# RMS norms of a diffusion backbone: the root's transpose reads a token's value by a stride of zero, and for queries and keys ScalarE writes the wide tile

## The chip, the cores and the metric

The kernel runs on one core of one Trainium2 chip. The time is the device time of one execution in microseconds (us); of several runs the median is given. The engines of the core work side by side, each through its own queue in order: TensorE (PE in the profile, its weight loads PEld), VectorE (DVE), ScalarE (ACT), GpSimd (POOL) and SyncE (SP), which issues the DMA transfers.

## The reference

Two layers over 512 latent tokens and 256 context tokens of width 1024, all in float32. Layer 0 is grouped-query attention with 16 query heads and 4 key/value heads of 64, layer 1 a bidirectional Mamba-2 mixer; a gated convolution FFN follows each. Every sub-layer begins with an RMS norm over the 1024 features of a token, and queries and keys are normed once more, over the 64 features of each head:

```python
def rms_norm(x, g):
    xf = x.astype(jnp.float32)
    y = xf * lax.rsqrt(jnp.mean(xf * xf, axis=-1, keepdims=True) + EPS)
    return (y * g.astype(jnp.float32)).astype(x.dtype)

q_l = rms_norm(q_l.reshape(bsz, seq, N_HEADS, HEAD_DIM), q_norm)
k_l = rms_norm(k_l.reshape(bsz, seq, N_KV_HEADS, HEAD_DIM), k_norm)
...
h_l = modulate(rms_norm(x, norm_ffn_w[i]), mod_l[3], mod_l[4])
```

The change concerns only how the reciprocal root of the mean square is brought from one number per token to a row that can be multiplied with the features.

## The kernel before

Activations lie transposed: features on the 128 partitions, tokens along the free dimension. A product of full float32 precision is three fast products of split operands (`split`, `mm3`): a high part rounded by ScalarE (L85), the rest by VectorE or GpSimd (L87), and on TensorE high with high, high with low, low with high (L105, L106, L108). TensorE is fed in this way from the first to the last stage: projections of queries, keys and values, attention by pairs of heads, output projection, FFN of layer 0, the Mamba mixer, FFN of layer 1.

`rstd_rows` is the common helper of all the norms. It takes the squares `sq`, sums them over the partitions with TensorE (tile `ss…`: tokens now on the partitions, `c` columns per block of 128 tokens; `c` is 1 for the norms over 1024 and 2 for a pair of heads), and works out the root on tiny tiles of 128 x (blocks times `c`): VectorE makes the mean plus epsilon (`a`, called `rsa` in the profile, L239), ScalarE the power -1/2 by a logarithm and an exponential (`y`, `rsy`, L241), VectorE a Newton step (`u`, `rsu`, L243 and L244). The last operation of the Newton step (L247) is done on VectorE at full width: it reads `u` and `y` with a stride of zero and writes `rb…`, a tile in which every value is repeated 128/c times. TensorE transposes `rb` in blocks of 128 x 128 (L253, into `rsT…`); each block comes out with the tokens along the free dimension and the value repeated over the partitions, so that it can be multiplied with the features.

The helper runs 21 times: for the attention input (`rsTa`, latent and context), for 2 pairs of key heads and 8 pairs of query heads over all 768 tokens (`rsTq`; called from `normed`, L529 to L540), in three segments each for the FFN of layer 0 and the Mamba input (`rsTf`, `rsTs`), once behind the Mamba scan (`rsTy`) and in two segments for the FFN of layer 1 (`rsTf`).

The order on the engines comes from a scheduler that simulates the program with its own costs, except in the first 60 us, where it is written by hand. Each engine then takes its instructions strictly in that order. Generators put the work of queries ahead of the pair that needs it: `normed` squares the query on ScalarE (L529), scales it (L530), swaps halves for the rotation by four DMAs (L533), rotates on VectorE or GpSimd (L534 to L536), and multiplies by `rsTq` (L540); ScalarE then splits it into `qh` (L85). In a pair, TensorE makes scores `ps_s` (L674, L676), ScalarE their exponential `pr` (L677), TensorE the products with the values `ps_o` (L638); for the next pair TensorE makes raw scores `ps_m` (L602), whose row maxima VectorE takes (L604). `ps_s` and `ps_m` share two PSUM buffers, used in turn.

Of the kernel before, what the change touches and what calls it, by code (L numbers as in the profile page):

```python
# [7 lines left out]
P = 128  # L8
# [3 lines left out]
ALU = mybir.AluOpType  # L12
# [55 lines left out]
def t3(g, name, dt=F32, n=T):  # L68
    return g.t3p.tile([P, n], dt, tag="t3", bufs=g.n3, name=name)
# [145 lines left out]
def follow(g, bi):  # L215

    if g.last_act is not None:
        g.tc.add_manual_dep(bi.ins, g.last_act.ins.name, mybir.DependencyInfo(
            mybir.DependencyClass.NoSync, mybir.DependencyReason.DATA), reason="order of tables")
    g.last_act = bi  # L220
# [6 lines left out]
def rstd_rows(g, sq, n, cols, width, name, bank):  # L227

    nc = g.nc
    c = cols.shape[-1]
    nt = n // P
    ps = bank(f"ss{name}")
    for t in range(nt):
        nc.tensor.matmul(ps[:, t * c : (t + 1) * c], sq[:, t * P : (t + 1) * P], cols, start=True, stop=True)
    small = lambda nm: g.p.tile([P, nt * c], F32, tag="rst", bufs=8, name=nm)
    a, y, u = small("rsa"), small("rsy"), small("rsu")
    nc.vector.tensor_scalar(a, ps[:, : nt * c], 1.0 / width, EPS, ALU.mult, ALU.add)  # L239

    for f in ((lambda: nc.scalar.activation(y, a, AF.Ln)), (lambda: nc.scalar.activation(y, y, AF.Exp, scale=-0.5))):  # L241
        follow(g, f()) if g.tables else f()
    nc.vector.tensor_tensor(u, y, a, ALU.mult)  # L243
    nc.vector.scalar_tensor_tensor(u, y, -0.5, u, ALU.mult, ALU.mult)  # L244
    rb = t3(g, f"rb{name}", n=n)
    wide = lambda v: v.unsqueeze(2).broadcast_to([P, nt * c, P // c])
    nc.vector.scalar_tensor_tensor(rb.rearrange("p (a b) -> p a b", b=P // c), wide(u), 1.5, wide(y), ALU.add, ALU.mult)  # L247
    yield BREAK
    out = []
    for t0 in range(0, nt, 4):  # L250
        pt = bank(f"rsT{name}")
        for t in range(t0, min(nt, t0 + 4)):
            nc.tensor.transpose(pt[:, (t - t0) * P : (t - t0 + 1) * P], rb[:, t * P : (t + 1) * P], g.ident)  # L253
        yield (pt, t0 * P, min(n, (t0 + 4) * P))


# [53 lines left out]
class Norm:  # L310
# [23 lines left out]
    def gen(self, seg, x, lag=2):  # L334

        i, a, b = seg
        g, nc, n = self.g, self.g.nc, b - a
        for _ in range(lag):
            yield
        rows = rstd_rows(g, self.acc[seg, 6], n, g.ones[:, :1], D, self.name, lambda nm: Bank(g, nm))  # L340
        next(rows)
        for _ in range(lag):
            yield
        rs = t3(g, f"rs{self.name}", n=n)
        nc.scalar.copy(rs, next(rows)[0][:, :n])
        for m in range(KT):
            modulated(g, self.h[i][m], x[i], rs, a, b, *self.a, self.streams[i][1], m,
                      pool=m in ((1, 4) if a else (1, 3, 5, 7)))
            yield
# [30 lines left out]
def attention(g, fill, X, late):  # L380
# [57 lines left out]
    for m in range(KT):  # L438
        sq = t2("sql") if m else acc
        nc.scalar.activation(sq, xs[0][m], AF.Square)  # L440
        if m:
            nc.vector.tensor_tensor(acc, acc, sq, ALU.add)
    norm = rstd_rows(g, acc, L, g.ones[:, :1], D, "a", Bk)
    g.qn8 = g.const.tile([P, 1], F32, name="qn8")
    nc.vector.tensor_scalar(g.qn8, g.par[:, PC["qn"] : PC["qn"] + 1], HD ** -0.5, None, ALU.mult)
# [23 lines left out]
    for m in range(KT):  # L469
# [11 lines left out]
        if m == 3:  # L481
            norm = rstd_rows(g, sqc, C, g.ones[:, :1], D, "a", Bk)
            next(norm)
# [960 lines left out]
```

## Time and profile before

| | us |
|---|---|
| median of 3 runs | 1902.63 |
| lowest and highest of them | 1900.31, 1909.34 |
| the profiled execution | 1901.6 |
| its span, first to last instruction | 1899.8 |
| VectorE's wide writes at L247 for queries and keys: 10 of 128 x 768 | 10.7 in all |
| the other eleven writes at L247 | 6.1 in all |
| TensorE idle in the span | 35.7 |

In the profile's rows a time comes first, then a duration, the engine, the line, the operation, the output and inputs by the program's names, and the shape. Brackets at the end give how long the engine sat idle before the instruction and what ended that idle time. Lines of groups give the busy time in us, the mean duration of one in ns, and the idle time before them.

### The profile page before, as it was taken

Reading aid. Unit: us, or ns where it says so; the run is one execution under the profiler, and the core shown is the slowest. Engines: PE = TensorE matmul, PEld = TensorE weight load, DVE = VectorE, ACT = ScalarE, POOL = GpSimd, SP = SyncE. Lnnn points to the kernel's source line nnn. Section 1 sums busy time; section 2 is a strip of 40 time slices with the busy share of each in tenths; the row PEclk is TensorE's granted clock in tenths of the full one; section 3 lists DMA queues with packets and bytes.
Section 4 is the critical chain, followed back from the end, with each engine's and each line's share of the span. In section 5 each row is a group of like instructions: output and inputs, shape, how many; then the busy total and the mean of one; then the engine's idle time right before and its main releaser. Section 6 shows DMA issues by size and latency. Waiting matters only on the chain.

```text
span 1899.8 us, 28697 instructions
## 1 busy us (share of the span) xinstructions
PE 1864.1 (98%) x11426; PEld 1548.5 (82%) x11426; DVE 1313.6 (69%) x1949; ACT 820.2 (43%) x1420; POOL 308.8 (16%) x268
## 2 busy tenths in 40 slices
PE   9899999999999999999999999999999999999999
PEld 7775564688888888888888888888887878888887
DVE  6578778678777776444487877777788466565555
ACT  4635344254222222222266676776666352323331
POOL 2241111040000000000041334444333210000000
PEclk9999999999999999999999999999999999999999
DMA  9221341014433553122223334434453223323232
GB/s 340 84 84 45 115 142 67 34 50 176 153 123 120 190 188 135 67 67 67 67 86 115 118 89 122 123 113 132 122 153 107 85 78 97 98 83 111 89 100 89
DMA packets 73430, 210.10 MB, mean 111 GB/s; under 512 B 8912, under 2 KB 14416, under 8 KB 73168
## 3 DMA queue, kind: packets, MB, share of 16 engines
q1 hardware_dynamic: 73296, 208.26, 33.7%
q8 instruction: 90, 1.47, 0.3%
q14 instruction: 44, 0.36, 0.1%
HBM read 198.79 MB, written 6.82 MB: 108 GB/s over the span
## 4 chain that ended last, share of the span: by engine, by line
PE 79%; DVE 10%; issue 4%; ACT 2%; DMA 2%; POOL 1%; SPq 0%; POOLq 0%; DVEq 0%; ACTq 0%
PE ps_up L106 10%; PE ps_up L108 10%; PE ps_up L105 10%; PE ps_d L105 6%; PE ps_d L106 6%; PE ps_d L108 6%; PE ps_in L108 4%; PE ps_in L106 4%; PE ps_in L105 4%; PE ps_o L638 2%; PE ps_s L674 2%; PE ps_st L1034 2%; DVE ht L281 1%; PE ps_wo L108 1%; PE ps_wo L105 1%
## 5 line engine op out<-in xcount | busy, mean ns | idle before, releaser
L87 DVE TENSOR_TENSOR wl<-wst,wh 128x1024 fp32r<-128x1024 f32 x205 | 258.1, 1259 | 238.7 <-PE ps_up L106 128.2
L85 ACT CAST wh<-wst 128x1024 fp32r<-128x1024 f32 x211 | 221.2, 1049 | 407.3 <-DMA wst<-in_wup 330.3
L106 PE MATMUL ps_up<-hlf,wh 128*128 128x512 f32 (+1 forms) x1008 | 357.0, 354 | 0.0
L108 PE MATMUL ps_up<-hhf,wl 128*128 128x512 f32 (+1 forms) x1008 | 356.8, 354 | 0.0
L105 PE MATMUL ps_up<-hhf,wh 128*128 128x512 f32 x1008 | 356.8, 354 | 0.0
L106 PEld LDWEIGHTS ps_up<-hlf,wh 128*128 128x128 f32 x1008 | 190.6, 189 | 26.4
L105 PEld LDWEIGHTS ps_up<-hhf,wh 128*128 128x128 f32 x1008 | 190.5, 189 | 26.5
L108 PEld LDWEIGHTS ps_up<-hhf,wl 128*128 128x128 f32 x1008 | 190.5, 189 | 26.3
L105 PE MATMUL ps_in<-hhs,wh 128*128 128x512 f32 (+1 forms) x560 | 204.4, 365 | 1.2 <-ACT dt L919 1.2
L106 PE MATMUL ps_in<-hls,wh 128*128 128x512 f32 (+1 forms) x560 | 199.3, 356 | 0.0
L108 PE MATMUL ps_in<-hhs,wl 128*128 128x512 f32 (+1 forms) x560 | 198.7, 355 | 0.0
L105 PE MATMUL ps_d<-hdh,wh 128*128 128x512 f32 (+1 forms) x568 | 193.4, 342 | 0.2 <-ACT hdh L85 0.2
L108 PE MATMUL ps_d<-hdh,wl 128*128 128x512 f32 (+1 forms) x568 | 193.5, 341 | 0.0
L106 PE MATMUL ps_d<-hdl,wh 128*128 128x512 f32 (+1 forms) x568 | 192.9, 340 | 0.3 <-DVE hdl L87 0.3
L785 DVE SCALAR_TENSOR_TENSOR X<-ps_d,mod,X 128x512 f32<-128x512 f32 (+1 forms) x224 | 124.3, 583 | 35.0 <-PE ps_d L108 34.8
L105 PEld LDWEIGHTS ps_in<-hhs,wh 128*128 128x128 f32 x560 | 105.9, 189 | 16.4 <-ACT dt L919 1.4
L106 PEld LDWEIGHTS ps_d<-hdl,wh 128*128 128x128 f32 x568 | 106.7, 188 | 14.8 <-DVE hdl L87 0.7
L108 PEld LDWEIGHTS ps_in<-hhs,wl 128*128 128x128 f32 x560 | 105.8, 189 | 14.7
L108 PEld LDWEIGHTS ps_d<-hdh,wl 128*128 128x128 f32 x568 | 106.7, 188 | 13.1
L105 PEld LDWEIGHTS ps_d<-hdh,wh 128*128 128x128 f32 x568 | 106.3, 188 | 13.6 <-ACT hdh L85 0.7
L106 PEld LDWEIGHTS ps_in<-hls,wh 128*128 128x128 f32 x560 | 106.0, 189 | 13.2
L677 ACT ACTIVATE pr<-ps_s 128x1024 f32<-128x1024 f32 x56 | 57.2, 1022 | 107.1 <-PE ps_s L676 106.2
(338 smaller groups left out, 3536.8 us busy)
## 6 DMA issues: line engine op xcount, KB each, us to landing
wst<-in_wup SPq DMA_DIRECT2D x88, 512.0 KB, 3.3
wada<-in_adaT SPq DMA_DIRECT2D x56, 512.0 KB, 3.4
wst<-in_win SPq DMA_DIRECT2D x48, 512.0 KB, 3.5
wst<-in_wdown SPq DMA_DIRECT2D x44, 512.0 KB, 3.7
E<-ad SPq DMA_DIRECT2D x64, 256.0 KB, 6.5
wada<-in_adaB SPq DMA_DIRECT2D x24, 512.0 KB, 4.2
ec<-ead SPq DMA_DIRECT2D x64, 128.0 KB, 5.2
wst<-in_wout SPq DMA_DIRECT2D x16, 512.0 KB, 3.4
```

Of the source, the lines that this page charges most:

```text
L85: keep(nc.scalar.copy(hi, src))
L87: keep(eng.tensor_tensor(lo, src, _r(hi), ALU.subtract))
L105: mm(out, wh, ah, start=first, stop=False)
L106: mm(out, wh, al, start=False, stop=False)
L108: mm(out, wl, ah, start=False, stop=last)
L281: nc.vector.scalar_tensor_tensor(t[:, c0:c1], ap, g.moda[layer][ca][:, m, v : v + 1], rs[:, c0:c1], ALU.mult, ALU.mult)
L638: nc.tensor.matmul(po[S64[e], :n], v, pr[:, 512 * e + off : 512 * e + off + n], start=first, stop=last)
L674: nc.tensor.matmul(outs[e], a[S64[e], k], b[S64[e], q], start=i == 0, stop=False)
L677: nc.scalar.activation(pr, ps, AF.Exp)
L785: nc.vector.scalar_tensor_tensor(ap, o[:, c0:c1], gate[:, m, v : v + 1], ap, ALU.mult, ALU.add)
L1034: nc.tensor.matmul(ps[:, d * 256 : (d + 1) * 256], Bt[:, t * P : (t + 1) * P], xw[d][t], start=t == ts[0], stop=t == ts[-1])
```

## The change

The Newton step's last operation becomes as small as the others: it writes the result into `a`, 128 x (blocks times `c`). Where `c` is 1, the transpose reads the column of `a` for a block of 128 tokens with a stride of zero, 128 times the same value, so no wide tile is written or allocated. Where `c` is 2 (queries and keys), the wide tile `rb` stays, and ScalarE writes it by a copy that reads `a` with a stride of zero (L248 of the changed kernel).

```diff
     nc.vector.tensor_tensor(u, y, a, ALU.mult)
     nc.vector.scalar_tensor_tensor(u, y, -0.5, u, ALU.mult, ALU.mult)
-    rb = t3(g, f"rb{name}", n=n)
-    wide = lambda v: v.unsqueeze(2).broadcast_to([P, nt * c, P // c])
-    nc.vector.scalar_tensor_tensor(rb.rearrange("p (a b) -> p a b", b=P // c), wide(u), 1.5, wide(y), ALU.add, ALU.mult)
+    nc.vector.scalar_tensor_tensor(a, u, 1.5, y, ALU.add, ALU.mult)
+    if c > 1:
+        rb = t3(g, f"rb{name}", n=n)
+        nc.scalar.copy(rb.rearrange("p (a b) -> p a b", b=P // c), a.unsqueeze(2).broadcast_to([P, nt * c, P // c]))
     yield BREAK
-    out = []
     for t0 in range(0, nt, 4):
         pt = bank(f"rsT{name}")
         for t in range(t0, min(nt, t0 + 4)):
-            nc.tensor.transpose(pt[:, (t - t0) * P : (t - t0 + 1) * P], rb[:, t * P : (t + 1) * P], g.ident)
+            nc.tensor.transpose(pt[:, (t - t0) * P : (t - t0 + 1) * P],
+                                a[:, t : t + 1].broadcast_to([P, P]) if c == 1 else rb[:, t * P : (t + 1) * P], g.ident)
         yield (pt, t0 * P, min(n, (t0 + 4) * P))
```

Lines below the edit move down by one. The scheduler also moves other instructions. Three places follow; names ending in a number are buffers, whose numbers differ between the two programs.

ScalarE in the first pair of heads, from its first exponential `pr` on. Here the root of the query in `raw_902` (before) is worked out while the query in `raw_903` (before) is squared. Before:

```order
L677 ACTIVATE pr<-ps_s 128x1024
L85 CAST wh<-wst 128x1024
L241 ACTIVATE rsy<-rsa 128x12
L241 ACTIVATE rsy<-rsy 128x12
L529 ACTIVATE qsq<-raw_903 128x768
L677 ACTIVATE pr<-ps_s 128x1024
L530 ACTIVATE raw_903<-raw_903,qn_241 128x768
L241 ACTIVATE rsy<-rsa 128x12
```

The same place after the change:

```order
L678 ACTIVATE pr<-ps_s 128x1024
L85 CAST wh<-wst 128x1024
L241 ACTIVATE rsy<-rsa 128x12
L241 ACTIVATE rsy<-rsy 128x12
L248 COPY rbq<-rsa 128x768
L530 ACTIVATE qsq<-raw_901 128x768
L678 ACTIVATE pr<-ps_s 128x1024
L531 ACTIVATE raw_901<-raw_901,qn_241 128x768
L241 ACTIVATE rsy<-rsa 128x12
```

The new copy stands directly behind the root's exponential and ahead of the next query's square and of the second `pr`. GpSimd just before that place, before the change (rotation of a query, then two low parts of weights):

```order
L534 TENSOR_TENSOR raw_902<-raw_902,cs 128x512
L535 TENSOR_TENSOR qsw<-qsw,cs 128x512
L536 TENSOR_TENSOR raw_902<-raw_902,qsw 128x512
L87 TENSOR_TENSOR wl<-wst,wh 128x1024 x2
L534 TENSOR_TENSOR raw_903<-raw_903,cs 128x512
```

and after it:

```order
L535 TENSOR_TENSOR raw_900<-raw_900,cs 128x512
L536 TENSOR_TENSOR qsw<-qsw,cs 128x512
L87 TENSOR_TENSOR wl<-wst,wh 128x1024
L537 TENSOR_TENSOR raw_900<-raw_900,qsw 128x512
L87 TENSOR_TENSOR wl<-wst,wh 128x1024
L535 TENSOR_TENSOR raw_901<-raw_901,cs 128x512
```

The first of the two weight operations has moved ahead of the rotation's last step.

ScalarE where the third pair of heads ends and the fourth begins, before:

```order
L647 ACTIVATE y<-ps_sum 128x512
L241 ACTIVATE rsy<-rsa 128x12
L648 ACTIVATE y<-y 128x512
L241 ACTIVATE rsy<-rsy 128x12
L85 CAST qh<-qs 128x768
L677 ACTIVATE pr<-ps_s 128x1024
L647 ACTIVATE y<-ps_oc 128x256
```

and after:

```order
L648 ACTIVATE y<-ps_sum 128x512
L241 ACTIVATE rsy<-rsa 128x12
L649 ACTIVATE y<-y 128x512
L241 ACTIVATE rsy<-rsy 128x12
L248 COPY rbq<-rsa 128x768
L85 CAST qh<-qs 128x768
L678 ACTIVATE pr<-ps_s 128x1024
L648 ACTIVATE y<-ps_oc 128x256
```

The copy of one query's root now stands ahead of the split of another query and of a `pr`.

TensorE in the norm ahead of the FFN of layer 0, at the second segment's transposes (`rsTf`), before:

```order
L105 MATMUL ps_first<-hhf_6_4041,wh 128x256
L253 MATMUL rsTf_4434<-cst,rbf_4403 128x128 x2
L105 MATMUL ps_d_4442<-hhol_3824,wh 128x256
L106 MATMUL ps_d_4442<-hlol_3825,wh 128x256
L108 MATMUL ps_d_4442<-hhol_3824,wl 128x256
```

and after:

```order
L105 MATMUL ps_first<-hhf_6_4049,wh 128x256
L106 MATMUL ps_first<-hlf_6_4050,wh 128x256
L108 MATMUL ps_first<-hhf_6_4049,wl 128x256
L253 MATMUL rsTf_4440<-cst,rsa 128x128 x2
L105 MATMUL ps_d_4448<-hhol_3832,wh 128x256
L106 MATMUL ps_d_4448<-hlol_3833,wh 128x256
```

Two products of the FFN's first tile now stand ahead of the transposes, and the transposes read `rsa`.

## The prediction, made before the changed kernel ran

> **What bounds the kernel now.** I read the page's busy times first, then the slices of clock and the chain that ended last, then TensorE's waits, and last the timeline at the places where those waits meet the change.
>
> ```profile
> PE 1864.1 (98%) x11426; PEld 1548.5 (82%) x11426; DVE 1313.6 (69%) x1949; ACT 820.2 (43%) x1420; POOL 308.8 (16%) x268
> PE 79%; DVE 10%; issue 4%; ACT 2%; DMA 2%; POOL 1%; SPq 0%; POOLq 0%; DVEq 0%; ACTq 0%
> PE ps_s L674 <- ACT pr L677: 3.0, 3, 1.7
> PE rsTq L253 <- DVE rbq L247: 2.7, 3, 1.2
> PE rsTf L253 <- DVE rbf L247: 0.9, 3, 0.4
> PE rsTs L253 <- DVE rbs L247: 1.0, 3, 0.4
> ```
>
> TensorE is busy for 98% and carries 79% of the chain: the kernel is bound by it nearly everywhere. So a saving on another engine counts only where TensorE waits. Its idle time is 1899.8 - 1864.1 = 35.7 us in all, and what it waits on the edited line (the wide write of VectorE, in us, times, longest) is 2.7 + 0.9 + 1.0 = 4.6 us. That caps the direct gain. The profiled execution took 1901.6 us, 1.0 below the median of the runs, 1902.63; I make the sum against the former and add it to the latter.
>
> **What is removed and added.**
>
> ```profile
> L247 DVE SCALAR_TENSOR_TENSOR rbq<-rsu,rsy 128x768 f32<-128x768 f32 x10 | 10.7, 1067 | 0.2
> L247 DVE SCALAR_TENSOR_TENSOR rbf<-rsu,rsy 128x256 f32<-128x256 f32 x5 | 2.6, 511 | 0.3
> L247 DVE SCALAR_TENSOR_TENSOR rbs<-rsu,rsy 128x256 f32<-128x256 f32 x3 | 1.7, 567 | 0.1
> L244 DVE SCALAR_TENSOR_TENSOR rsu<-rsy,rsu x21: 159/163/1250, 13.6 to 1535.6; 128x12 f32<-128x12 f32 x10, 128x2 f32<-128x2 f32 x9, 128x4 f32<-128x4 f32 x2
> L85 ACT CAST qh<-raw 128x768 fp32r<-128x768 f32 x4 | 3.3, 829 | 3.9 <-DVE raw L540 3.9
> ACT pr L677 <- PE ps_s L676: 106.2, 44, 6.1
> ```
>
> VectorE's 21 wide writes become small operations like L244's, 0.163 us at the median. It is relieved of 10.7 - 1.6 = 9.1 us in the attention stage. ScalarE gains ten copies; it has no such copy yet, but its cast of the same 128 x 768 takes 0.829 us, so 8.3 us. In the chain of a query's root the exchange is even: 0.16 + 0.83 against 0.96 at most places, plus one handover. ScalarE's spare time is ample on the whole (its exponentials waited 106.2 us for TensorE between 60 and 400 us). But its queue is in order: the copy waits for VectorE's Newton step, and whatever stands behind the copy waits too. That decides the sign.
>
> **Place 1, first pair, 115 to 121 us.**
>
> ```profile
> 114.90 1.05 ACT L85 CAST wh<-wst 128x1024 fp32r<-128x1024 f32 x1 [0.70 <-POOL wl L87]
> 116.21 0.83 ACT L529 ACTIVATE qsq<-raw 128x768 f32<-128x768 f32 x1
> 116.94 1.00 ACT L677 ACTIVATE pr<-ps_s 128x1024 f32<-128x1024 f32 x1
> 116.33 2.07 DVE L243 TENSOR_TENSOR rsu<-rsy,rsa 128x12 f32<-128x12 f32 x1 [1.26 <-ACT rsy L241]
> 118.64 0.96 DVE L247 SCALAR_TENSOR_TENSOR rbq<-rsu,rsy 128x768 f32<-128x768 f32 x1
> 116.02 2.35 POOL L87 TENSOR_TENSOR wl<-wst,wh 128x1024 fp32r<-128x1024 f32 x1 [1.16 <-ACT wh L85]
> 115.76 0.39 PE L602 MATMUL ps_m<-kh,qh 64*128 64x512 f32 x2
> 117.08 2.72 PE L236 MATMUL ssq<-cst,qsq 128*128 128x2 f32 x12 [0.94 <-ACT qsq L529]
> ```
>
> TensorE already waits 0.94 us here for the square of the next query. In the changed order the copy stands ahead of that square. VectorE's L243, twelve elements wide, takes 2.07 us instead of 0.17, ending as GpSimd's subtraction ends. So the small result exists only at 118.64 + 0.16 = 118.80; copy to 119.65, square to 120.5, and TensorE's sums start there, not at 117.08: +3.4 us, with nothing else in its queue. The changed order on GpSimd frees ScalarE's cast of its 0.70 us wait, and all of it starts that much earlier: +2.7. If GpSimd's operation fell elsewhere, the Newton step would be done at about 116.9, square at 118.6: +1.5. I take **+2.7**, bounds +1.5 to +3.4.
>
> [...]
>
> **Place 2, third to fourth pair, 207 to 213 us.**
>
> ```profile
> 207.95 0.82 ACT L85 CAST qh<-qs 128x768 fp32r<-128x768 f32 x1
> 210.02 1.02 ACT L677 ACTIVATE pr<-ps_s 128x1024 f32<-128x1024 f32 x1 [1.25 <-PE ps_s L676]
> 210.43 0.96 DVE L247 SCALAR_TENSOR_TENSOR rbq<-rsu,rsy 128x768 f32<-128x768 f32 x1
> 210.92 0.50 PE L602 MATMUL ps_m<-kh,qh 64*128 64x256 f32 x4
> 212.36 0.50 PE L674 MATMUL ps_s<-qh,kh 64*128 64x512 f32 x2
> ```
>
> VectorE comes to the root at 210.43. The copy then ends at 210.6 + 0.83 = 211.45, the split of the query that was done at 208.77 ends at 212.3, and `pr` runs from 212.3 to 213.3 instead of 210.02 to 211.04. The next `ps_s` needs the buffer that `pr` reads, so it starts at 213.35, not 212.36: **+1.0**, bounds +0.4 (only the raw scores wait for `qh`) to +1.4.
>
> **Place 3, 288 to 293 us.**
>
> ```profile
> 287.91 1.02 ACT L677 ACTIVATE pr<-ps_s 128x1024 f32<-128x1024 f32 x1 [0.34 <-PE ps_s L676]
> 290.91 0.94 DVE L247 SCALAR_TENSOR_TENSOR rbq<-rsu,rsy 128x768 f32<-128x768 f32 x1
> 291.92 1.12 PE L253 MATMUL rsTq<-cst,rbq 128*128 128x128 f32 x4 [0.54 <-DVE rbq L247]
> 292.96 0.79 PE L674 MATMUL ps_s<-qh,kh 64*128 64x512 f32 x2
> ```
>
> Here the copy is scheduled ahead of the `pr` that ran at 287.91; it ends at 291.07 + 0.83 = 291.9, `pr` at 292.95, and the next `ps_s` starts at 293.0, as before. But the four transposes, which filled that wait, now come later: **+0.4**, bounds 0 and +1.5 (if VectorE's queue slips by one 1.2 us operation).
>
> **Place 4, a gain from VectorE's relief.**
>
> ```profile
> 131.58 0.96 DVE L247 SCALAR_TENSOR_TENSOR rbq<-rsu,rsy 128x768 f32<-128x768 f32 x1
> 136.55 0.50 PE L602 MATMUL ps_m<-kh,qh 64*128 64x512 f32 x2 [1.19 <-DVE ma L604]
> ```
>
> TensorE waits 1.19 us for VectorE's maxima, and the wide write stands ahead of them in the same queue: 0.96 - 0.16 = **-0.8**, bounds -1.2 and 0. The other six copies I take at 0: transposes wait for a root at two more places only, both in the 2.7 us above, and there the chain keeps its length; at worst a copy's 0.83 us each, +5.0.
>
> **The norms over 1024.**
>
> ```profile
> 402.73 0.44 PE L253 MATMUL rsTf<-cst,rbf 128*128 128x128 f32 x2 [0.23 <-DVE rbf L247]
> 415.06 0.44 PE L253 MATMUL rsTf<-cst,rbf 128*128 128x128 f32 x2 [0.42 <-DVE rbf L247]
> 1538.41 0.50 PE L105 MATMUL ps_first<-hhf,wh 128*128 128x256 f32 x2 [1.17 <-ACT hhf L290]
> L1145 PEld LDWEIGHTS ps_end<-acsT,cst x4: 185/189/190, 1022.3 to 1022.7; 128*128 128x128 f32 x4
> L236 PEld LDWEIGHTS ssq<-cst,qsq x120: 186/192/338, 69.3 to 283.3; 128*128 128x128 f32 x120
> ```
>
> Each root is there 0.43 - 0.16 = 0.27 us sooner. In the two norms with three segments that takes away about 0.23, 0.3 and 0.1 of the waits shown (0.9 and 1.0 in all; VectorE's order puts another operation ahead at the third): -0.6 each. In the last norm the wait is further down the chain, at the modulated rows, and shrinks by 0.27 in each of two segments: -0.5. At the start and behind the Mamba scan TensorE waits for none of it: 0. Together **-1.7**, bounds -3.0 and 0. The weight load with a stride of zero costs nothing, by the one that exists: L1145 loads a column 128 times over in 0.189 us, a dense load of L236 takes 0.192.
>
> **The sum**: +2.7 + 1.0 + 0.4 - 0.8 - 1.7 = +1.6 us; 1902.6 + 1.6, that is **1904.2 us**. The bounds of the places add up to -2.3 and +11.3.
>
> **Rivals.** *The stall also halves the clock (slower).*
>
> ```profile
> 117.00:124.00 7.00, 6.92 (x68) 5.15 (x72) 6.08 (x9) 3.86 (x7) 1.38 (x1) 0.53 0.29 85
> 286.00:300.00 14.00, 10.96 (x54) 5.25 (x54) 12.42 (x13) 4.87 (x6) 3.75 (x3) 0.76 0.26 103
> ```
>
> The third number from a row's end is the granted clock: 0.53 over 7 us here, right behind a wait, and 0.76 over 14 us around place 3 (1 is full speed). That is a loss of 0.47 x 7 = 3.3 and of 0.24 x 14 = 3.4 us. If the longer stalls at places 1 to 3 each bring one more such stretch, with the six copies at half their bound, the sum is 1.6 + 3 x 2 + 2.5 = +10, 1912.7. For it: the dips stand where TensorE waits. Against: place 1's stretch is slow already, and idle time in it is not lost twice. It decides from two added stretches on. [...]
>
> *The relief wins (faster).* GpSimd's operation misses L243, place 2 is absorbed, the norms save their full waits: +1.5 + 0.4 + 0 - 1.2 - 3.0 = -2.3, so 1900.3; with both slow stretches above gone, 6.7 less, 1893.6. For it: VectorE is busy 69%. Against: TensorE hardly waits for it.
>
> *Zero-stride transposes are slow.* The transposing form has never been loaded so here. If its loads took the slowest of L236, 0.338 instead of 0.14, 26 of them cost 5 us more: about 1909. L1145 speaks against it.
>
> **How the numbers follow.** Forecast 0.60, slower rival 0.17, faster rival 0.18, slow transposes 0.05. A measurement of this kernel tells about 0.5%, 9.5 us, from no change: below 1893.1 counts as faster, above 1912.1 as slower. The slower rival crosses the upper line in two thirds of its cases (0.11), the forecast in one of twenty (0.03, six copies at their bound), slow transposes in a third (0.02): 0.16 slower. The faster rival crosses the lower one in under half, where both stretches go (0.08). That leaves 0.76 for no change. The range runs from 1895, the faster rival with most of those stretches gone, to 1913, the slower rival; for the forecast alone it is 1901 to 1908.
>
> **What would show it.** Right: a wait of 3 to 4 us of TensorE for `qsq` at 117 us; `ps_s` waiting for `pr` near 212; no waits of `rsTf` and `rsTs` for VectorE; ScalarE's copies at 0.83 us; zero-stride loads at 0.14. Wrong: ScalarE's copy never waiting for VectorE, or dips of the clock where there were none.

## The result and the profile after

| | before | with the change |
|---|---|---|
| median of 20 runs each, us | 1901.28 | 1907.82 |
| lowest and highest | 1899.22, 1909.34 | 1902.84, 1913.87 |
| the profiled execution, its span | 1901.6, 1899.8 | 1909.78, 1907.9 |

The changed kernel is slower by a ratio of 1.0032 (95% interval 1.0023 to 1.0041), that is 6.1 us. The prediction was 1904.2. The profiled execution of the change lies 2.0 us above the median of its runs, that of before 0.3, so the two traces differ by 8.1 us and the runs by some 6. One execution of the kernel called "all copies late" below took 8853 us and is left out of its ratio, though not of its median.

Busy times of the engines, from the page of the changed kernel:

```profile
PE 1866.8 (98%) x11426; PEld 1552.8 (81%) x11426; DVE 1304.2 (68%) x1949; ACT 828.8 (43%) x1430; POOL 305.8 (16%) x268
```

VectorE is relieved by 9.4 us, ScalarE has 8.6 more. ScalarE's part is as worked out (8.3). VectorE's is less: the working had 9.1 for attention alone, but the ten small last steps there took 3.9 us (0.39 each in the mean, since three of them took 0.31 to 1.25 us) and not 1.6, which leaves 10.7 - 3.9 = 6.8. And the modulated rows `ht` of the norms over 1024, 48 operations of 530 to 533 ns before, take 608 to 611 ns with the change, 3.8 us in all; why is not shown. TensorE's idle time goes from 35.7 to 1907.9 - 1866.8 = 41.1 us: 5.4 of the 8.1. The other 2.7 is TensorE being busy longer with the same 11426 matmuls, which fits the clock (granted 0.993 in the mean of this execution against 0.994 in that of before, and below). TensorE's waits with the change (line, what it waited for, us, times, longest):

```profile
PE rsTq L253 <- ACT rbq L248: 4.1, 3, 2.0
PE ssq L236 <- ACT qsq L530: 3.5, 1, 3.5
PE ps_m L603 <- ACT qh L85: 3.2, 4, 1.8
PE ps_s L675 <- ACT pr L678: 3.0, 3, 1.7
PE ps_first L106 <- POOL hlf L289: 2.6, 5, 1.0
PE ps_in L105 <- ACT dt L920: 1.7, 1, 1.7
PE ps_first L106 <- POOL hls L289: 1.0, 2, 0.7
```

At the roots of queries and keys ScalarE has taken VectorE's place as what TensorE waits for. The waits of `rsTf` and `rsTs` for the wide tile are gone from the list, and the same norms' waits for GpSimd's low parts are longer (`hlf`, 2.6 against 1.3 us) or new (`hls`).

Where the time went can be read from the start of the same work in both timelines (the first instruction on TensorE that writes the tile named; us):

| stretch | before | change | difference |
|---|---|---|---|
| start to the first `ssq` (a key's sums) | 69.4 | 71.7 | +2.3 |
| to the first scores `ps_s` | 42.5 | 48.4 | +5.9 |
| to the first `ps_o` | 7.8 | 10.4 | +2.6 |
| rest of attention, to the first `ssf` | 280.0 | 277.2 | -2.8 |
| the norm of FFN 0, `ssf` to `ps_up` | 31.0 | 31.1 | +0.1 |
| the norm of Mamba, `sss` to `ps_in` | 39.7 | 40.5 | +0.8 |
| the norm of FFN 1, `ssf` to `ps_up` | 17.7 | 16.9 | -0.8 |

So everything is lost before 131 us, in the first queries and the first pair, and the norms over 1024 together gave nothing. The -0.8 of the last norm is not all the stride's: before, a slow stretch of the clock stood in it, and here it does not (mean granted clock 0.91 from 1521 to 1539 us before, 1.00 from 1529 to 1547).

**The stretch to `ps_o` (place 1)**, timeline of the changed kernel, ScalarE, VectorE, GpSimd and TensorE (start, duration, instruction, idle time before it and what ended it):

```profile
122.25 1.04 ACT L85 CAST wh<-wst 128x1024 fp32r<-128x1024 f32 x1
123.36 2.37 POOL L87 TENSOR_TENSOR wl<-wst,wh 128x1024 fp32r<-128x1024 f32 x1 [0.45 <-ACT wh L85]
123.68 2.07 DVE L243 TENSOR_TENSOR rsu<-rsy,rsa 128x12 f32<-128x12 f32 x1 [0.45 <-ACT rsy L241]
126.20 0.83 ACT L248 COPY rbq<-rsa 128x768 f32<-128x768 f32 x1 [2.54 <-DVE rsa L245]
126.93 0.84 ACT L530 ACTIVATE qsq<-raw 128x768 f32<-128x768 f32 x1
127.82 2.72 PE L236 MATMUL ssq<-cst,qsq 128*128 128x2 f32 x12 [3.52 <-ACT qsq L530]
```

ScalarE stands still for 2.54 us inside the queue, at its copy, because VectorE's twelve-element operation takes 2.07 us, where the next two take 0.17 each, and ends at 125.75 us, 0.02 us after GpSimd's subtraction (125.73). The square of the next query is behind the copy, its input ready since 96 us, and TensorE waits for the square: 3.52 us.

**The stretch to `ps_s`** holds what I had not foreseen, at the root of the second pair's query:

```profile
100.42 0.37 ACT L524 COPY v<-ps_v 128x256 f32<-128x256 f32 x1 [2.79 <-PE ps_v L522]
100.69 1.05 ACT L85 CAST wh<-wst 128x1024 fp32r<-128x1024 f32 x1
101.64 0.21 ACT L241 ACTIVATE rsy<-rsa 128x12 f32<-128x12 f32 x1
101.94 1.23 DVE L605 TENSOR_REDUCE ma<-ps_m 128x2 f32<-128x1024 f32 x1 [2.16 <-PE ps_m L603]
103.12 1.29 POOL L535 TENSOR_TENSOR raw<-raw,cs 128x512 f32<-128x512 f32 x1 [13.03 <-DMA qsw<-raw]
103.27 1.16 DVE L244 SCALAR_TENSOR_TENSOR rsu<-rsy,rsu 128x12 f32<-128x12 f32 x1
104.47 1.18 DVE L245 SCALAR_TENSOR_TENSOR rsa<-rsu,rsy 128x12 f32<-128x12 f32 x1
105.69 0.83 ACT L248 COPY rbq<-rsa 128x768 f32<-128x768 f32 x1 [3.59 <-DVE rsa L245]
106.57 0.66 PE L253 MATMUL rsTq<-cst,rbq 128*128 128x128 f32 x4 [2.03 <-ACT rbq L248]
```

The same root before:

```profile
90.60 1.03 ACT L85 CAST wh<-wst 128x1024 fp32r<-128x1024 f32 x1
93.96 0.37 ACT L523 COPY v<-ps_v 128x256 f32<-128x256 f32 x1 [2.33 <-PE ps_v L521]
94.92 0.17 DVE L244 SCALAR_TENSOR_TENSOR rsu<-rsy,rsu 128x12 f32<-128x12 f32 x1
95.91 1.32 POOL L534 TENSOR_TENSOR raw<-raw,cs 128x512 f32<-128x512 f32 x1 [12.16 <-DMA qsw<-raw]
96.00 1.22 DVE L604 TENSOR_REDUCE ma<-ps_m 128x2 f32<-128x1024 f32 x1
96.39 0.60 PE L253 MATMUL rsTq<-cst,rbq 128*128 128x128 f32 x4
```

The new order has a cast of weights between the values' copy and the root's logarithm (before, it stood ahead of the copy), so the root starts 1.05 us later. VectorE's order has changed as well: a maximum of 1.23 us (101.94), which before followed the wide write, now stands ahead of the Newton step. The step has hardly begun when GpSimd's rotation of the very same query starts: two of VectorE's tiny operations last 1.16 and 1.18 us instead of 0.17, each ending 0.02 us after a step of the rotation (103.27 + 1.16 against 103.12 + 1.29, 104.47 + 1.18 against 104.37 + 1.26). Only then can ScalarE copy. TensorE waits 2.03 us for it, where before it waited for nothing.

**The clock.** Windows of both kernels, of before first (the third number from the end is the granted clock):

```profile
60.00:65.00 5.00, 5.00 (x28) 4.27 (x27) 1.20 (x4) 4.87 (x13) 2.54 (x4) 1.00 0.01 2
76.00:84.00 8.00, 7.07 (x62) 6.86 (x62) 7.23 (x11) 4.75 (x8) 2.71 (x1) 1.00 0.85 263
116.50:124.00 7.50, 6.92 (x68) 5.15 (x72) 6.58 (x9) 4.36 (x7) 1.88 (x1) 0.54 0.27 79
```

and with the change:

```profile
60.00:65.00 5.00, 4.71 (x13) 3.50 (x14) 2.19 (x5) 3.70 (x9) 1.70 (x3) 0.66 0.01 2
78.00:86.00 8.00, 7.68 (x38) 7.45 (x38) 3.27 (x9) 1.88 (x6) 0.00 (x0) 0.57 0.57 171
126.00:136.50 10.50, 8.68 (x82) 6.39 (x84) 3.40 (x9) 6.24 (x9) 0.00 (x0) 0.51 0.34 107
```

Two slow stretches are new, 0.34 x 5 = 1.7 and 0.43 x 8 = 3.4 us: 5.1 of the 8.2 us that the stretches to the first `ps_s` lost. The one behind place 1 is about 10 us long instead of 7 (0.49 x 10.5 / 0.5 and 0.46 x 7.5 / 0.5, at half speed: the granted clock is 0.50 from 127 to 136 us with the change and from 117 to 123 before, and the twelve sums `ssq` take 2.72 us in both against 1.50 at 1.00, at 113.3 us before). Two slow stretches of before, near 290 and 1530 us, are half as long or gone in this execution (granted clock from 276 to 312 us 0.95 against 0.91, from 1529 to 1547 us 1.00 against 0.91). Whether that is the change or chance, one execution can't tell. The first new stretch stands in none of the twelve traces of the experiments below (the granted clock from 60 to 65 us is 1.00 in all). A slow stretch between 74 and 86 us stands in seven of them, three of which have no copy on ScalarE and are no slower than before; so it is not the mark of that copy. The mean clock over all runs says more, and is compared further below.

### The profile page after: what moved, and what is told of

It reads as the page before. It is cut to its first block, busy times and chain, and to the rows that moved or that the text cites. A ratio compares the mean times of both kernels' runs of the same rounds, so it can differ in the third digit from the quotient of the medians.

```text
span 1907.9 us, 28702 instructions
## 1 busy us (share of the span) xinstructions
PE 1866.8 (98%) x11426; PEld 1552.8 (81%) x11426; DVE 1304.2 (68%) x1949; ACT 828.8 (43%) x1430; POOL 305.8 (16%) x268
## 5 line engine op out<-in xcount | busy, mean ns | idle before, releaser
L106 PE MATMUL ps_up<-hlf,wh 128*128 128x512 f32 x1008 | 357.0, 354 | 0.0
L108 PE MATMUL ps_up<-hhf,wl 128*128 128x512 f32 x1008 | 356.8, 354 | 0.0
```

The costliest lines, as they stand in the source:

```text
L106: mm(out, wh, al, start=False, stop=False)
L108: mm(out, wl, ah, start=False, stop=last)
```

## The experiments

Ratios are to the kernel before on the same chip, with the 95% interval; 7 to 20 runs each.

| kernel | median, us | ratio |
|---|---|---|
| the change | 1907.82 | 1.0032 (1.0023 to 1.0041) |
| the copy alone | 1911.24 | 1.0042 (1.0026 to 1.0058) |
| the stride alone | 1902.12 | 0.9997 (0.9987 to 1.0007) |
| all copies late | 1902.46 | 0.9996 (0.9984 to 1.0007) |
| place 1's copy late | 1903.99 | 1.0011 (1.0002 to 1.0021) |
| the nine others late | 1905.21 | 1.0015 (0.9999 to 1.0030) |
| before, wide write late | 1901.98 | 1.0001 (0.9993 to 1.0010) |
| VectorE copies | 1903.95 | 1.0001 (0.9990 to 1.0013) |
| VectorE copies, late | 1900.33 | 0.9990 (0.9981 to 0.9998) |
| the same again | 1900.19 | 0.9988 (0.9977 to 0.9998) |
| no Newton step, ScalarE copies | 1896.28 | 0.9969 (0.9958 to 0.9981) |
| the same again | 1897.99 | 0.9960 (0.9944 to 0.9975) |
| no Newton step, VectorE copies | 1904.52 | 0.9990 (0.9973 to 1.0008) |

**The two halves of the change.** In the first kernel the norms over 1024 keep VectorE's wide write, in the second the queries and keys do. The first has the change's order in attention and the order of before behind it, the second the reverse.

The first, against the kernel before:

```diff
-    nc.vector.scalar_tensor_tensor(rb.rearrange("p (a b) -> p a b", b=P // c), wide(u), 1.5, wide(y), ALU.add, ALU.mult)
+    if c > 1:
+        nc.vector.scalar_tensor_tensor(a, u, 1.5, y, ALU.add, ALU.mult)
+        nc.scalar.copy(rb.rearrange("p (a b) -> p a b", b=P // c), wide(a))
+    else:
+        nc.vector.scalar_tensor_tensor(rb.rearrange("p (a b) -> p a b", b=P // c), wide(u), 1.5, wide(y), ALU.add, ALU.mult)
```

> The copy of ScalarE for queries and keys alone; the norms over 1024 write their wide tile on VectorE as before. Theory (all of the loss is the copy's place in ScalarE's queue, between 60 and 130 us): 1906 to 1909 us, as the full change, with TensorE waiting 3.5 us for the next query's square and about 4 us for the wide tile. Rival 1 (half of the loss comes from the transposes with a stride of zero): 1903 to 1905. Rival 2 (the waits cost little and the clock's dips are drawn anew in every kernel): the waits as in the full change, but any time from 1900 to 1910.

> The transposes with a stride of zero for the norms over 1024 alone; queries and keys as before. Theory: the waits for the wide tiles of these norms go, others take their place, and the time is that of before within 1 us (1900.5 to 1902.5). My prediction's term: 1.7 us less, 1899.6. Rival 1 (slow loads): 1904 or more, with weight loads of the transposes above 0.2 us.

Measured: 1.0042 and 0.9997. All of the loss is ScalarE's copy (its median, of 7 runs, is 2 us over my upper bound, its interval reaches down to the full change). TensorE's waits are the expected ones: 3.5 us for the next query's square and 5.0 for the wide tile. The stride of zero costs nothing, and gains nothing that 12 runs can tell: the 1.7 us of my term lie inside the interval, but the three stretches of the norms add up to 88.4 us in its trace (31.1 + 40.2 + 17.1) as before (31.0 + 39.7 + 17.7). The stride alone has the same exchange of waits as the full change; TensorE's list for it:

```profile
PE ps_first L106 <- POOL hlf L291: 2.2, 4, 1.0
PE ps_in L105 <- ACT dt L922: 1.7, 1, 1.7
PE ps_first L105 <- ACT hhf L293: 1.4, 2, 1.0
PE ps_first L106 <- POOL hls L291: 1.1, 2, 0.7
```

Before, the first two were 1.3 and 1.2, and there were 0.9 and 1.0 of waits for the wide tiles: what the sooner root gives is waited for elsewhere in the same norms. Only the last norm is shorter, by 0.5 us (17.7 to 17.1, with the granted clock at 0.91 from 1521 to 1539 us in both traces), as its part of the term had it; the Mamba norm is longer by as much.

**The copy's place in ScalarE's queue.** The copy is written behind the helper's pause, so the scheduler puts the squares of the next queries ahead of it.

```diff
     nc.vector.scalar_tensor_tensor(a, u, 1.5, y, ALU.add, ALU.mult)
-    if c > 1:
-        rb = t3(g, f"rb{name}", n=n)
-        nc.scalar.copy(rb.rearrange("p (a b) -> p a b", b=P // c), a.unsqueeze(2).broadcast_to([P, nt * c, P // c]))
     yield BREAK
+    if c > 1:
+        rb = t3(g, f"rb{name}", n=n)
+        nc.scalar.copy(rb.rearrange("p (a b) -> p a b", b=P // c), a.unsqueeze(2).broadcast_to([P, nt * c, P // c]))
```

> The full change, but ScalarE's copy is written behind the helper's first pause, so that the scheduler puts the squares of the next queries ahead of it. Theory (an in-order queue: what stands behind the copy waits for VectorE): the wait of 3.5 us for the square is gone, and 2.5 to 4 us of the loss with it, 1902 to 1905. If the loss is the copy's length alone and not its place: 1907 as in the full change.

Measured: 0.9996. The wait for the square is gone, and all of the loss with it, some 7 us (1.0032 - 0.9996), where I had expected 2.5 to 4. The timeline at the root near 100 us shows the other part of it:

```profile
98.95 0.22 ACT L241 ACTIVATE rsy<-rsa 128x12 f32<-128x12 f32 x1
99.65 0.17 DVE L244 SCALAR_TENSOR_TENSOR rsu<-rsy,rsu 128x12 f32<-128x12 f32 x1
100.06 0.83 ACT L249 COPY rbq<-rsa 128x768 f32<-128x768 f32 x1 [0.65 <-DVE rsa L245]
101.01 1.28 POOL L535 TENSOR_TENSOR raw<-raw,cs 128x512 f32<-128x512 f32 x1 [13.82 <-ACT rbq L249]
```

The cast of weights is ahead of the values' copy again, VectorE's maximum behind the Newton step; the root is done before GpSimd's rotation starts, and the tiny operation lasts 0.17 us.

**One place against the other nine.** A parameter of the helper decides which copies are written late; the first kernel delays that of place 1 only, the second all but that one.

```diff
-        yield from normed(qs, g.qn8, eng)
+        yield from normed(qs, g.qn8, eng, p == 2)
```

> The full change with one copy of ten moved: that of the query whose root is worked out at the place of the 3.5 us wait, behind the helper's pause, so that the next query's square stands ahead of it. Every other engine keeps its order but for a few instructions. Theory (this stall is the largest single piece and costs its own length beyond the 0.94 us of before, plus what the halved clock behind it takes): 1903 to 1905.5 us, the wait for the square gone and the mean clock of the runs nearer to 0.995 than to 0.993. Rival 1 (the wait only moves: TensorE waits as long a little later, in the same pair): 1906.5 or more. Rival 2 (the loss lies in the key and query norms ahead of it, before 110 us): 1906 or more, though the wait is gone.

> The counterpart: the full change with the nine other copies moved behind the pause, this one left where the change has it. Theory: the wait of 3.5 us for the square stays, the wait of 2.0 us for the wide tile near 105 us goes (the cast of weights stands ahead of the values' copy again, so the root comes ahead of GpSimd's rotation and no small operation of VectorE lasts 1.2 us): 1904.5 to 1907. Rival 1 (all of the loss is the one stall): 1907 to 1909. Rival 2 (it lies in the other nine): 1901.5 to 1903.5.

Measured: 1.0011 and 1.0015, 1904.0 and 1905.2 us, both within the theory's ranges, and the pieces add up: place 1 is worth 1.0032 - 1.0011 = 0.0021, the nine others 1.0032 - 1.0015 = 0.0017, both together 1.0032 - 0.9996 = 0.0036. With intervals of 0.0009 to 0.0015 to either side, each piece is known to within 0.001 to 0.002 only. TensorE's waits for the square, of the first kernel and then of the second:

```profile
130.00 1.88 PE L236 MATMUL ssq<-cst,qsq 128*128 128x2 f32 x12 [1.44 <-ACT qsq L533]
```

```profile
123.71 2.72 PE L236 MATMUL ssq<-cst,qsq 128*128 128x2 f32 x12 [4.31 <-ACT qsq L533]
```

Place 1's copy cost 0.0021 x 1902 = 4.0 us, though its wait shrank by 3.52 - 1.44 = 2.1. My expectation that the wait would be gone was wrong: it shrank. In the second kernel the wait of 2.03 us near 105 us is gone as expected, and one of 1.92 us for a wide tile at 84.0 us is new. With place 1's copy late the mean clock rose from 0.9929 to 0.9940 (halfway to the 0.995 that I had expected it to be near), and over the 20 runs of the change 0.001 of mean clock goes with 1.24 us: another 1.4 us, roughly.

**The engine of the copy.** VectorE makes the copy from the small result, at the change's place and behind the pause; and, as a control, the kernel before with its wide write behind the pause.

```diff
-        nc.scalar.copy(rb.rearrange("p (a b) -> p a b", b=P // c), a.unsqueeze(2).broadcast_to([P, nt * c, P // c]))
+        nc.vector.tensor_copy(rb.rearrange("p (a b) -> p a b", b=P // c), a.unsqueeze(2).broadcast_to([P, nt * c, P // c]))
```

> The full change, but VectorE makes the copy with a stride of zero for queries and keys, from the small result. Theory (ScalarE's queue is the cause): no wait for a square, and the time of before plus at most 10 x 0.16 us for the added small operations where they lie on the path: 1901 to 1903.5. If the split of the last step into a small operation and a copy is the cause, whatever the engine: 1906 to 1908.

> The full change with VectorE making the copy, behind the helper's pause: an attempt at a version that beats both. VectorE's copy took 0.56 us against 0.96 for the wide Newton step, ScalarE has no copy in its queue. Theory: no wait for a square, the time of before or up to 2 us less, 1899.5 to 1902.5. Rival: the copy, now behind other operations of VectorE, makes the transposes late: 1903.5 or more.

> The late copy on VectorE a second time, on the same chip as the two others: if its gain of 0.1% is real, a ratio of 0.998 to 0.9995 again; if it was the spread of the runs, 0.9995 to 1.001.

> The kernel before with VectorE's wide write for queries and keys moved behind the helper's pause, nothing else. It tells what the pause gives by itself in the two kernels with a late copy. If the late place alone makes a better order: 1 to 3 us less than before, 1899 to 1901. If not: before within 1 us, and the gain of the late copy on VectorE is the shorter operation.

Measured: at the change's place 1.0001, so the split into a small operation and a copy costs nothing by itself that these runs can tell (the median, 1903.95, is just over my upper bound; the ratio is not). Behind the pause it is 0.9990 and 0.9988, twice just below 1 with the whole interval: the one version of the same computation that beats both kernels, the one before by some 2 us. The control is 1.0001, so for VectorE's write the late place is no better order in itself, which speaks against the pause as the reason of the recovery on ScalarE too. What the gain of 2 us comes from is open. The copy is shorter at the median (0.56 us, below, against 0.958 for the wide Newton step), but the longest took 2.695 us: the ten take 9.3 us, and with the ten small last steps (3.9) that is more than the 10.7 of before. The mean clock of the runs is 0.0008 and 0.0006 above that of before on the same chip, which by the 1.24 us for each 0.001 goes with 1.0 and 0.8 us of the gain.

```profile
L249 DVE COPY rbq<-rsa x10: 552/560/2695, 73.7 to 290.4; 128x768 f32<-128x768 f32 x10
```

**The wait inside the copy, or its length.** For queries and keys the Newton step is left out, so ScalarE's copy reads ScalarE's own exponential, at the place that the change gives it; and the same with VectorE's copy as a control.

```diff
+    if c > 1:
+        a = y
+    else:
-    nc.vector.tensor_tensor(u, y, a, ALU.mult)
-    nc.vector.scalar_tensor_tensor(u, y, -0.5, u, ALU.mult, ALU.mult)
-    nc.vector.scalar_tensor_tensor(a, u, 1.5, y, ALU.add, ALU.mult)
+        nc.vector.tensor_tensor(u, y, a, ALU.mult)
+        nc.vector.scalar_tensor_tensor(u, y, -0.5, u, ALU.mult, ALU.mult)
+        nc.vector.scalar_tensor_tensor(a, u, 1.5, y, ALU.add, ALU.mult)
```

> The full change without the Newton step for queries and keys (left out: the three small operations of VectorE), so ScalarE's copy reads ScalarE's own exponential and waits for no other engine. The copy stands where the change puts it, ahead of the next query's square. Theory (what costs is that the queue waits for VectorE inside the copy, 2.5 and 3.6 us at the two places, less its 0.83 us length): the wait for the square is 2 us or less, the wait of 2.0 us for the wide tile near 105 us is gone, 1900 to 1903.5 us. Rival (the copies' own length ahead of other work is the cost): the waits shrink by no more than 1 us, 1905 or more.

> The control of the run without the Newton step: again the step is left out for queries and keys, but VectorE makes the wide copy. With the Newton step, ScalarE's copy cost 0.3% against VectorE's (1.0032 against 1.0001 of before). Theory (ScalarE's copy costs because its queue waits for VectorE inside it): without that wait the two engines are equal within 0.1%, so 1894.5 to 1898.5 here. Rival (ScalarE's copy costs by its place, wait or not): VectorE's copy is 4 to 6 us better than the 1896.3 of ScalarE's, 1890 to 1892.5.

> ScalarE's copy without the Newton step once more, on the same chip as its control: 1895 to 1898, 0.2 to 0.4% less than before.

Measured: 0.9969 and 0.9960 with ScalarE's copy, 0.9990 with VectorE's. So a copy on ScalarE at the very same place is 0.2 to 0.3% *better* than one on VectorE, as soon as it waits for no other engine. The rival (the copy's place, wait or not) falls. TensorE's waits for the wide tile of queries and keys, 4.1 us with the change, are gone from both lists (one of 0.3 is left with VectorE's copy). My theory had the sign right and two numbers wrong: ScalarE's run came out 2 to 4 us below its range, and the control, which shares the shorter chain, was not equal to it but 6.5 us slower on the same chip. Place 1 of the run with ScalarE's copy:

```profile
116.05 2.35 POOL L87 TENSOR_TENSOR wl<-wst,wh 128x1024 fp32r<-128x1024 f32 x1 [1.16 <-ACT wh L85]
116.36 0.83 ACT L251 COPY rbq<-rsy 128x768 f32<-128x768 f32 x1
117.10 0.84 ACT L533 ACTIVATE qsq<-raw 128x768 f32<-128x768 f32 x1
117.99 1.96 PE L236 MATMUL ssq<-cst,qsq 128*128 128x2 f32 x12 [1.82 <-ACT qsq L533]
```

and of the control with VectorE's:

```profile
116.74 2.35 POOL L87 TENSOR_TENSOR wl<-wst,wh 128x1024 fp32r<-128x1024 f32 x1 [1.16 <-ACT wh L85]
117.05 2.46 DVE L251 COPY rbq<-rsy 128x768 f32<-128x768 f32 x1 [1.26 <-ACT rsy L241]
117.80 2.04 PE L236 MATMUL ssq<-cst,qsq 128*128 128x2 f32 x12 [0.94 <-ACT qsq L533]
```

GpSimd's subtraction runs in both. ScalarE's copy takes its 0.83 us beside it; VectorE's takes 2.46 us and ends at 119.51, 0.42 us after GpSimd's (119.09). With ScalarE the wait for the square is 1.82 us, of which the copy's length is about 0.8 more than the 0.94 of before: that is the whole price of the copy's length at its worst place. The long copy of the control costs TensorE nothing at this place: its wait for the square is the 0.94 us of before. Where ScalarE's copy is the better one is farther on: in the two profiles of one chip the spans differ by 4.8 us, and the stretch from the first `ps_o` to the first `ssf` by 5.2 (277.2 against 282.4). What makes the difference there was not taken apart; in all, the ten copies take 11.0 us on VectorE against some 8.3 on ScalarE.

## Why the prediction was right, and where it was off

The sign, the range and the mechanism held: the time is 1907.8 against a range of 1895 to 1913, ScalarE's in-order queue decides, and the largest single wait stands where the prediction put it. The size did not hold: the sum was +1.6 and the runs show +6.1. The wide range owes its width to the rivals; for the forecast alone it was 1901 to 1908, and the result lies at its upper end. Places 1 and 2 are right by their mechanism and size; place 3 itself fell by 1.4 where a rise was worked out, the norms gave nothing, and some of the errors cancel. By its steps:

| step of the prediction | predicted, us | measured, us |
|---|---|---|
| place 1 (copy ahead of the next square) | +2.7 | 0.94 to 3.52: +2.6 |
| place 2 (copy ahead of a split and of `pr`) | +1.0 | 0.82 + 0.42 new: +1.2 |
| place 3 | +0.4 | 3.1 to 1.7: -1.4, and +1.3 in the 20 us behind it |
| place 4 (VectorE's maxima) | -0.8 | 1.19 to none: -1.2 |
| the other six copies | 0, up to +5.0 | +2.0 at 106.6, +0.5 at 95.7 |
| norms over 1024 | -1.7 | +0.1 (by the stretches above) |
| halved clock | a rival of its own | +2.7 in the profiles |

Place 2 as it came, with the change; all four rows are where the working had put them, ten microseconds later:

```profile
220.78 0.83 ACT L248 COPY rbq<-rsa 128x768 f32<-128x768 f32 x1 [2.58 <-DVE rsa L245]
221.51 0.83 ACT L85 CAST qh<-qs 128x768 fp32r<-128x768 f32 x1
222.39 0.50 PE L603 MATMUL ps_m<-kh,qh 64*128 64x256 f32 x4 [0.82 <-ACT qh L85]
223.32 0.50 PE L675 MATMUL ps_s<-qh,kh 64*128 64x512 f32 x2 [0.42 <-ACT pr L678]
```

- **The other six copies** are the step that failed most. I took them at 0 because "the chain keeps its length". The chain of instructions does; but the order moved a cast of 1.05 us on ScalarE and a maximum of 1.23 us on VectorE into it, that brought it under GpSimd's rotation, and there VectorE's two tiny operations cost 2.0 us more. I had seen this effect at place 1 and not asked where else a root now meets GpSimd. The run with the nine others late prices these six and places 2 to 4 together at 0.0017, some 3.2 us.
- **The norms** were sized by the wait that was removed, not by what is late next. The next wait (GpSimd's low parts, `dt` of the Mamba input: 1.2 to 1.7 us) took what the first two norms had gained; only the last kept its 0.5 (the stride alone, above).
- **The clock** was put into a rival with 0.17. It is no alternative to the forecast but a surcharge that can come with a stall of it: the mean over 20 runs is 0.9929 against 0.9944 over the 106 runs of before that were made beside the experiments (0.9936 to 0.9948 in its four sets), which by the 1.24 us for each 0.001 is about 2 of the 6.1 us (the chips differ, so roughly). It follows ScalarE's early copies: 0.9907 for the copy alone, 0.9927 with only place 1's early, 0.9940 with the nine others early, 0.9945 with all late, each against 0.9947 or 0.9948 of before on its chip. Of the three added stretches of the rival one came, behind place 1 (some 10 us instead of 7); the two new ones lie ahead of it, and its number, 1912.7, did not come.
- The zero-stride loads were rightly taken at nothing: 0.134 us against 0.141 for those of the wide tile. The faster rival had its two mechanisms right (place 4, and VectorE's relief) and not their weight.
- VectorE's relief was taken from the median of a small operation, 0.163 us. Ten of them took 3.9 us and not 1.6: the mean counts here, because the long ones are far above the median, up to 1.249 us.
- Of the signs listed, the wait for `qsq` (3.5 us, ten microseconds later than said), the wait of `ps_s` for `pr` (0.42 us, at 223), the waits of `rsTf` and `rsTs` gone, the copies at 0.83 us and the loads at 0.13 us all came. "Dips of the clock where there were none" came too, which I had listed as against the forecast.

## What to carry to other kernels

Moving an operation to an idle engine paid where its input was made there too: ScalarE's copy gained 0.2 to 0.3% over VectorE's when it read ScalarE's own result, and cost 0.3 to 0.4% when it had to wait for VectorE in an in-order queue with other work behind it. Where the copy must wait for another engine, put it behind what is ready, or leave it where its input is made: a late copy on VectorE beat the kernel before by 0.1%. And price a shorter chain by the wait that comes next, not by the one that it removes.

## What the runs showed of the hardware that I had not expected

- A VectorE operation on twelve elements took far longer beside some GpSimd operations: the 21 of L243 took 0.149 us at the least and 2.071 at the most with the change. Of the thirty operations of the Newton step for queries and keys (L243 to L245), twenty took 0.16 or 0.17 us, and ten took 0.28 to 2.07 us, each of these ending 0.01 to 0.03 us after a GpSimd operation that ran beside it. VectorE's copy, which has one input, varied as well: 0.552 to 2.695 us in the late copy's run (the row above), and 2.46 us where it ended 0.42 us after GpSimd's subtraction. ScalarE's ten copies took 0.824 to 0.833 us, three of them beside a GpSimd operation (at 105.7, 143.8 and 268.2 us). Why the one engine's operations grow longer and the other's do not was not shown.
- The granted clock fell to half (0.50 from 79 to 85 us with the change) behind a wait of about 1 us, and not each time: behind 1.18 us for `rsTq` at 74.8 us before it stays at 1.00, behind 1.13 us for the same transposes at 77.2 us with the change there is a slow stretch of some 7 us. What sets one off was not shown. So one execution's clock says little about a change, and the mean over the runs is what was compared here.
